# Maxima of the attention scores from 64-row products in pairs, with the decay taken off by VectorE, in the second half of a forgetting attention

## The chip, the cores and the metric

The kernel runs on one core of a Trainium2 chip. A core has five engines with a queue of instructions each: TensorE (matrix products, from SBUF into PSUM), VectorE, ScalarE and GpSimd (elementwise work and reductions), and SyncE, here called SP, which only issues DMA transfers. In the profile they are PE (and PEld for TensorE's loads of the stationary operand), DVE, ACT, POOL and SP. An engine works through its queue in order; a semaphore makes an instruction wait for one of another engine or for a DMA. The metric is device time in microseconds (us) of one execution, as the median of several runs. Everything is float32 outside; products are made in fp32r, with a number split into a high and a low part where more digits are needed.

## The reference

One layer of a hybrid encoder on 2,048 frames plus 16 learned meta tokens (T = 2,064), width 1,024: a normalisation, one input projection, three groups of heads side by side (a gated linear recurrence, a forgetting attention with 8 heads of 64, an RWKV-7 recurrence), an output projection, and a feed-forward part of width 2,816. The change lies in the forgetting attention:

```python
log_f = jax.nn.log_sigmoid(f_logit + f_bias)
c = jnp.cumsum(log_f, axis=1).transpose(0, 2, 1)          # decay, one row a head
s = jnp.einsum('bhqd,bhkd->bhqk', qb, kh) + (cb[..., :, None] - c[..., None, :])
s = jnp.where(kpos[None, :] <= qpos[:, None], s, -jnp.inf)
p = jax.nn.softmax(s, axis=-1)
return jnp.einsum('bhqk,bhkd->bhqd', p, vh)
```

A softmax needs the maximum of each query's row of scores, or a number near it, before the exponentials. The term of the query, cb, is the same for a whole row, so that maximum is the one of (q k - c of the key) over the keys up to the query.

## The kernel before

The stages follow one another: the input projection with the two recurrences beside it, then attention, then the rest of the output projection, then the feed-forward part. The program is traced in Python and a planner (`schedule_with_timeline_sim=True`) then sets the order of each engine's queue by a simulated timeline, the order of the program's text and the buffers that come free; `issue_after` and `add_manual_dep` give it further edges. So instructions of the output projection (tiles `pswo`, lines 172 to 174, three products for each split product) stand between those of attention wherever the planner saw room, as soon as their blocks of 128 frames are ready.

`Attn` (from line 439) works in two halves: blocks 0 and 1 of 512 queries for all 8 heads, then blocks 2 and 3 for all 8 heads. A unit is one head and one block. `run` (line 802) makes a head's keys, then for each block the maxima, and at the same time the weights of the unit two before (AHEAD = 2).

`keys` (line 500) loads for a head: `k1`, 128 rows, the high part of the keys above their low part, and `k2`, the high part in rows 0 to 63, a row of ones (64), and the negative decay as two rows, `ch` and `cl` (65 and 66). In the first half keys number at most `KHALF` = 1,040 and a buffer holds two heads; in the second half a head has 2,064 and fills one of two buffers.

`maxima` (line 530) loads three forms of the block's queries: `q3` (queries in rows 0 to 63, constants 0, 1, 1 in rows 64 to 66, zero below), `q1` (queries twice) and `q2` (their low part, a row for the shift below). For each 128 queries it goes over pieces of keys cut at 0, 400, 912, 1424, 1936 and 2064 (`MAX_CUTS`), up to the last key that these queries may see: one product of `q3` and `k2` over all 128 rows (line 554), which holds the decay by its extra rows; for the last piece a bf16 product that adds the causal mask (line 556); and a VectorE reduction to the maximum of each query (line 559). Block 2 has 13 pieces, block 3 has 17. Then the maxima of a query are joined, turned into a row (line 567) and written negated into row 64 of `q2` (line 568), so that the scores come out shifted.

`weights` (line 649) makes for each 128 keys the scores by two products over 128 rows (lines 681 and 682), the exponential on ScalarE (686), a triangular mask on GpSimd (688), the sums of weights on GpSimd and VectorE (725), and the products with the values (704). These are made in groups of up to eight instructions; each uses 64 of the array's columns (`tile_position=(0, at)`), two of them at the same time, with a manual edge so that both can start together. Between two score tiles `fill` lets as many pieces of the maxima run as their share demands.

PSUM: the maxima, the row transposes and the row totals take turns in three banks in most of the kernel (`mx`, line 493). Loads and stores go through SP's queue, in order.

## Time and profile before

| | |
|---|---|
| median of 3 runs | 3062.89 us (3059.62 to 3063.98) |
| the profiled execution | 3063.42 us, its span 3061.7 us |
| busy, whole span | TensorE 95%, VectorE 67%, ScalarE 48%, GpSimd 45% |
| mean granted TensorE clock | 0.971 |
| reductions to maxima (line 559) | 352, 190.2 us in all |
| products for maxima (line 554) | 352 over both halves |
| value products (line 704) | 704, from 934.6 to 1569.0 us |

The span is from the first to the last instruction. A busy TensorE is not one at its peak: the records of matrix products overlap, so starts are compared where a product's cost matters. A waiting row (A <- B) names the instruction that waited and what ended its wait. "issue" means that the profile shows no engine or transfer that ended it.

### The profile page before, as it was taken

To read this page: it belongs to the slowest core of one execution; us is meant where nothing else is said; L and a number is where in the kernel's file an instruction comes from. 1 tells how busy PE (TensorE), PEld (TensorE's weight loads), DVE (VectorE), ACT (ScalarE), POOL (GpSimd) and SP (SyncE) were. 2 spreads that over 40 slices of the span, in tenths; PEclk is the share of its full clock that TensorE was granted. 3 is DMA by queue.
4 is the path that set the end of the run, shared out by engine and by line. 5 is a ranking of instruction groups with operands and counts; after the bars stand their busy time and mean duration, and the time that the engine had idled before them with its cause. 6 is when DMAs were issued, how large, how long until landed. Compare 5 with 4: busy or idle time off the path is not lost.

```text
span 3061.7 us, 52809 instructions
## 1 busy us (share of the span) xinstructions
PE 2910.2 (95%) x18694; PEld 2487.6 (81%) x18694; DVE 2057.7 (67%) x3934; ACT 1479.1 (48%) x2853; POOL 1365.7 (45%) x1599
## 2 busy tenths in 40 slices
PE   6998999999989999999999899999999999999998
PEld 6997898888876654566568899999999999787786
DVE  5268645656677785555636888888778777547766
ACT  4245332434346554454534656666566665324333
POOL 1001121122214556566843457445645544556765
PEclk8999999999989898999999999999999999999999
DMA  6776478466654347434336555566677765535454
GB/s 216 244 234 207 163 240 292 154 199 205 211 156 92 88 105 211 109 100 122 75 94 206 171 181 180 172 202 213 209 215 212 220 192 165 171 102 175 148 162 145
DMA packets 467750, 532.58 MB, mean 174 GB/s; under 512 B 85550, under 2 KB 355576, under 8 KB 465932
## 3 DMA queue, kind: packets, MB, share of 16 engines
q1 hardware_dynamic: 466716, 528.27, 56.5%
q8 instruction: 147, 2.41, 0.3%
q14 instruction: 119, 0.97, 0.1%
q0 software_dynamic: 768, 0.93, 0.1%
HBM read 369.11 MB, written 159.95 MB: 173 GB/s over the span
## 4 chain that ended last, share of the span: by engine, by line
PE 34%; DVE 5%; DMA 5%; POOL 3%; issue 3%; ACT 1%; SPq 0%; POOLq 0%; DVEq 0%; ACTq 0%
PE psu L172 8%; PE psu L173 8%; PE psu L174 8%; PE psd L172 2%; PE psd L173 2%; PE psd L174 2%; DMA u<-scr_ff 2%; DMA xt<-scr_h 1%; DVE uw L1603 1%; PE pswo L172 1%; PE pswo L174 1%; PE pswo L173 1%; DVE fo L1603 1%; DVE uy L1738 1%; POOL u L1858 1%
## 5 line engine op out<-in xcount | busy, mean ns | idle before, releaser
L172 PE MATMUL psu<-xo,uw 128*128 128x344 f32 x1848 | 590.8, 323 | 14.7 <-DVE vb L1787 6.9
L173 PE MATMUL psu<-xo,uw 128*128 128x344 f32 x1848 | 593.1, 321 | 0.0
L174 PE MATMUL psu<-xo,uw 128*128 128x344 f32 x1848 | 584.3, 320 | 1.5 <-DVE uw L1603 1.5
L172 PE MATMUL psp<-xh,wh 128*128 128x384 f32 (+2 forms) x1152 | 383.5, 333 | 4.5 <-ACT wh L166 3.0
L174 PE MATMUL psp<-xh,wl 128*128 128x384 f32 (+2 forms) x1152 | 379.5, 330 | 2.6 <-DMA wl<-scr_wk 2.5
L173 PE MATMUL psp<-xl,wh 128*128 128x384 f32 (+2 forms) x1152 | 379.3, 329 | 0.0
L1603 DVE TENSOR_TENSOR uw<-uq,uw 128x512 fp32r<-128x512 f32 x341 | 321.0, 947 | 65.1 <-ACT uw L1602 62.8
L172 PEld LDWEIGHTS psu<-xo,uw 128*128 128x128 f32 x1848 | 347.4, 189 | 19.2 <-DVE vb L1787 9.4
L174 PEld LDWEIGHTS psu<-xo,uw 128*128 128x128 f32 x1848 | 347.2, 189 | 2.4 <-DVE uw L1603 2.3
L173 PEld LDWEIGHTS psu<-xo,uw 128*128 128x128 f32 x1848 | 348.5, 189 | 0.1
L1602 ACT ACTIVATE uw<-uq 128x512 fp32r<-128x512 f32 x462 | 287.5, 627 | 107.5 <-PE psu L174 46.6
L686 ACT ACTIVATE p<-sc,bias 128x512 f32<-128x512 f32 (+4 forms) x352 | 197.0, 589 | 194.9 <-PE sc L682 162.1
L559 DVE TENSOR_REDUCE mc<-mx 128x1 f32<-128x512 f32 (+6 forms) x352 | 190.2, 564 | 114.1 <-PE mx L554 87.2
L1738 DVE SCALAR_TENSOR_TENSOR uy<-psu,ffn_cols,uy 128x342 f32<-128x342 f32 (+1 forms) x396 | 223.7, 567 | 62.3 <-ACT uy L1736 60.9
L1744 POOL TENSOR_TENSOR uy<-uy,uy 128x342 f32<-128x342 f32 (+1 forms) x132 | 140.0, 1061 | 252.7 <-DVE uy L1738 70.1
L725 POOL TENSOR_TENSOR acc<-acc,p 128x512 f32<-128x512 f32 (+3 forms) x208 | 221.7, 1068 | 53.1 <-DVE acc L725 23.9
L1603 POOL TENSOR_TENSOR uw<-uq,uw 128x512 fp32r<-128x512 f32 x121 | 177.6, 1468 | 148.0 <-ACT uw L1602 129.5
L172 PEld LDWEIGHTS psp<-xh,wh 128*128 128x128 f32 x1152 | 221.7, 192 | 11.6 <-issue 4.2
L174 PEld LDWEIGHTS psp<-xh,wl 128*128 128x128 f32 x1152 | 220.8, 192 | 12.0 <-issue 5.7
L173 PEld LDWEIGHTS psp<-xl,wh 128*128 128x128 f32 x1152 | 221.3, 192 | 7.5 <-issue 5.4
L1603 DVE TENSOR_TENSOR fo<-u,fo 128x896 fp32r<-128x896 f32 x88 | 109.0, 1240 | 118.8 <-ACT fo L1602 118.8
L1602 ACT ACTIVATE fo<-u 128x896 fp32r<-128x896 f32 x88 | 81.1, 922 | 200.9 <-POOL u L1859 103.8
(470 smaller groups left out, 6470.3 us busy)
## 6 DMA issues: line engine op xcount, KB each, us to landing
uq<-scr_us SPq DMA_DIRECT2D x220, 256.0 KB
uq<-in_ffn_up_dram SPq DMA_DIRECT2D x209, 256.0 KB
wl<-scr_wk SPq DMA_DIRECT2D x48, 512.0 KB
wh<-scr_wk SPq DMA_DIRECT2D x48, 512.0 KB
u<-scr_ff SPq DMA_DIRECT2D x88, 256.0 KB
scr_ff<-uy SPq DMA_DIRECT2D x110, 171.0 KB
raw<-in_w_in_dram SPq DMA_DIRECT2D x24, 512.0 KB
scr_wk<-wh SPq DMA_DIRECT2D x24, 512.0 KB
```

Source lines behind the costliest of these rows:

```text
L172: nc.tensor.matmul(out, ah, bh, start=first, stop=False, skip_group_check=more)
L173: nc.tensor.matmul(out, ah, bl, start=False, stop=False, skip_group_check=more)
L174: nc.tensor.matmul(out, al, bh, start=False, stop=last, skip_group_check=more)
L559: self.reduced = nc.vector.tensor_reduce(mc[:rows, i, ci : ci + 1], ps[:rows, : e - a], axis=AX.X, op=ALU.max)
L686: last = nc.scalar.activation(p[:rows, :w], ps[:rows, :w], AF.Exp, bias=bias[:rows, j : j + 1])
L725: eng.tensor_tensor(a, ps_[0][0][:rows, c0:n] if start and i == 1 else a, p[:rows, : n - c0], op=ALU.add)
L1602: core.nc.scalar.activation(hi, src, AF.Copy)
L1603: (eng or core.nc.vector).tensor_tensor(lo, src, hi, op=ALU.subtract)
L1738: stt(y[:, :n], src[:, i : n + i], cw[:, 44 * i + cc : 44 * i + cc + 1], y[:, :n], op0=ALU.mult, op1=ALU.add)
L1744: core.pooled = nc.gpsimd.tensor_tensor(v[:, :n], g[:, :n], v[:, :n], op=ALU.mult)
L1858: tt(s3, a0, b0, op=ALU.subtract)
```

## The change

In the second half of attention only (keys that number more than 1,040):

- The product for a piece of maxima uses 64 rows: `q1` and `k1` in rows 0 to 63, or `q1` and `k2` in rows 64 to 127, where `k2` now holds the high part of the keys. Two pieces that follow one another form a pair, one on each half of the rows (`tile_position=(lo, 0)`), in two PSUM banks. A manual edge makes the first product of a pair wait also for the reader of the second one's bank. An odd last piece of a block is alone. The mask's product is made behind the pair.
- The decay is no longer part of the product. It is loaded from a new scratch row `c`, the same for all 128 partitions, in three stretches a head (keys 0 to 911, 912 to 1423, 1424 to 2063), and VectorE's reduction becomes `tensor_tensor_reduce`: it subtracts the decay from the PSUM piece, writes it back, and gives the maximum. The first stretch has two places that heads use in turn; the two others have one place each. One of the two places is the room of the three `q3` tiles, which the second half needs no more; the other is a new tile of 1,552 columns.
- `q3` isn't loaded in the second half, and `ch` and `cl` only for the first 1,040 keys. The two later stretches of decay are issued on SP behind the query loads of the head's first block.

In both halves `q2`, `q3` and `k2` have their rows exchanged: the constant rows are 0 to 63, queries and keys 64 to 127. In the first half the pieces are made as before. The output tile of the meta tokens shares a tag with another tile.

```diff
@@ gate_block
+    nc.sync.dma_start(scr["c"][:, t0 : t0 + n], c)
     ch, cl = new("k", F32R), new("r", F32R)
...
+    if t0 < KHALF:
+        w = min(n, KHALF - t0)
+        nc.sync.dma_start(scr["ch"][:, t0 : t0 + w], ch[:, :w].bitcast(F32))
+        nc.sync.dma_start(scr["cl"][:, t0 : t0 + w], cl[:, :w].bitcast(F32))
@@ Attn.mx
         self.bank = (self.bank + 1) % 3 if self.wide else 0
+        self.taken += self.bank != 2
+        self.at = 2 if self.bank == 2 else self.taken % 2
@@ Attn.keys
-        nc.sync.dma_start(k2f[0:64, :n], scr["kh"][r, :n])
-        g = 64 + self.ONES
-        nc.sync.dma_start(k2f[g : g + 1, :n], scr["ch"][h : h + 1, :n])
-        nc.sync.dma_start(k2f[g + 1 : g + 2, :n], scr["cl"][h : h + 1, :n])
+        spans = []
+        if n <= KHALF:
+            nc.sync.dma_start(k2f[1:2, :n], scr["ch"][h : h + 1, :n])
+            nc.sync.dma_start(k2f[2:3, :n], scr["cl"][h : h + 1, :n])
+        else:
+            spans = self.spans(n)
+
+            def span(i):
+                t, a, e = spans[i]
+                nc.sync.dma_start(t, scr["c"][h : h + 1, a:e].broadcast_to([P, e - a]))
+
+            span(0)
+            self.rest.extend(lambda i=i: span(i) for i in range(1, len(spans)))
         nc.sync.dma_start(k1f[0:64, :n], scr["kh"][r, :n])
+        nc.sync.dma_start(k2f[64:128, :n], scr["kh"][r, :n])
         nc.sync.dma_start(k1f[64:128, :n], scr["kl"][r, :n])
...
+    def spans(self, n):
+
+        self.parity ^= 1
+        if not self.decay:
+            own = self.own.tile([P, 1552], F32, tag="decay", name=self.core.n("decay"), bufs=1)
+            self.decay = [self.q3[:].rearrange("p i t -> p (i t)").bitcast(F32), own]
+        homes = (self.parity, 0, 0, 912), (0, 912, 912, 1424), (1, 912, 1424, n)
+        return [(self.decay[i][:, o : o + e - a], a, e) for i, o, a, e in homes]
@@ Attn.maxima
-        nc.sync.dma_start(q3[0:64, :n].bitcast(F32), scr["qh"][r, ts])
+        q3 = None if spans else self.next("q3")
+        if not spans:
+            nc.sync.dma_start(q3[64:128, :n].bitcast(F32), scr["qh"][r, ts])
         nc.sync.dma_start(q1[0:64, :n].bitcast(F32), scr["qh"][r, ts])
         nc.sync.dma_start(q1[64:128, :n].bitcast(F32), scr["qh"][r, ts])
-        nc.sync.dma_start(q2[0:64, :n].bitcast(F32), scr["ql"][r, ts])
+        nc.sync.dma_start(q2[64:128, :n].bitcast(F32), scr["ql"][r, ts])
+        while self.rest:
+            self.rest.pop(0)()
...
+        for g in range(0, len(pieces) if spans else 0, 2):
+            pair, banks, first = [], [], None
+            for piece in pieces[g : g + 2]:
+                pair.append((self.mx(), *piece))
+                banks.append(self.at)
+            for k, lo, (ps, i, ci, a, e, qo, rows, prior) in zip((k1, k2), (0, 64), pair):
+                mm = nc.tensor.matmul(
+                    ps[:rows, : e - a], q1[lo : lo + 64, qo : qo + rows], k[lo : lo + 64, a:e],
+                    start=True, stop=e < prior + rows, tile_position=(lo, 0),
+                )
+                if first is None and len(pair) > 1 and self.readers.get(banks[1]):
+                    core.tc.add_manual_dep(
+                        mm.ins, self.readers[banks[1]],
+                        mybir.DependencyInfo(mybir.DependencyClass.Sync, mybir.DependencyReason.DATA),
+                        reason="both of a pair at the same time",
+                    )
+                first = mm
+            for ps, i, ci, a, e, qo, rows, prior in pair:
+                if e == prior + rows:
+                    nc.tensor.matmul(
+                        ps[:rows, prior - a : e - a], core.identb[:], core.futureb[:], start=False, stop=True
+                    )
+            for at, (ps, i, ci, a, e, qo, rows, prior) in zip(banks, pair):
+                c = next(t[:rows, a - x : e - x] for t, x, y in spans if x <= a < y)
+                self.reduced = nc.vector.tensor_tensor_reduce(
+                    ps[:rows, : e - a], ps[:rows, : e - a], c, 1.0, NEG, ALU.subtract, ALU.max,
+                    mc[:rows, i, ci : ci + 1],
+                )
+                self.readers[at] = self.reduced.ins.name
+            for _ in pair:
+                yield None
...
-        nc.scalar.activation(q2[64:65], ps[0:1], AF.Identity, scale=-1.0, bias=core.ncref[:, ref, h : h + 1])
+        nc.scalar.activation(q2[0:1], ps[0:1], AF.Identity, scale=-1.0, bias=core.ncref[:, ref, h : h + 1])
```

More of the change, by code (lines that the diff above doesn't have):

```diff
@@ L547, in maxima @@
         nc.vector.memset(mc[:], NEG)
-        for i, (qo, rows, prior) in enumerate(qt):
-            for ci in range(len(MAX_CUTS) - 1):
-                a, e = MAX_CUTS[ci], min(MAX_CUTS[ci + 1], prior + rows)
-                if a >= e:
-                    break
-                ps, last = self.mx(), e == prior + rows
-                nc.tensor.matmul(ps[:rows, : e - a], q3[:, qo : qo + rows], k2[:, a:e], start=True, stop=not last)
-                if last:
+        pieces = [
+            (i, ci, x, min(y, prior + rows), qo, rows, prior)
+            for i, (qo, rows, prior) in enumerate(qt)
+            for ci, (x, y) in enumerate(zip(MAX_CUTS, MAX_CUTS[1:])) if x < prior + rows
+        ]
@@ L656, in weights @@
         nc, core, scr = self.nc, self.core, self.scr
-        k1, k2, v1 = keys
+        k1, k2, v1, _ = keys
         q1, q2, bias = queries
@@ L800, with run @@
     AHEAD = 2
-    def run(self, pool):
-        self.queue = self.nc.sync
+    def run(self, pool, own):
+        self.queue, self.own = self.nc.sync, own
         ready = []
@@ L2085, in hybrid_block_kernel @@
             pool(p1b, "pad", 1, **right).tile([P, 24832], F32, name="pad")
-            at.run(pool(p1b, "mt", 1, **right, **early))
+            at.run(*(pool(p1b, s, 1, **right, **early) for s in ("mt", "decay")))
     qp = pool(ctx, "qp", 1, **early)
```

48 lines of the change are left out of this document (27 added, 21 removed).

## The prediction

> **What bounds the kernel now.** I read the page's head first, then the instructions of the value products' line for where attention ends, then the table of windows for its second half (1140 to 1570 us), then the waits of that stretch, then TensorE's instructions in order of time.
>
> ```profile
> span 3061.7 us, 52809 instructions
> ```
>
> ```profile
> L704 PE MATMUL po<-p,v x704: 203/592/1117, 934.6 to 1569.0; 128*64 128x512 f32 x112, 128*64 128x144 f32 x17, 16*64 16x16 f32 x16, 128*64 128x400 f32 x16
> ```
>
> ```profile
> core 0: us, PE busy (x) PEld busy (x) DVE busy (x) ACT busy (x) POOL busy (x), PEclk, DMA share, GB/s
> 1140.00:1215.00 75.00, 66.21 (x306) 34.40 (x305) 45.36 (x100) 33.75 (x62) 39.54 (x47) 0.89 0.74 207
> 1215.00:1300.00 85.00, 81.53 (x362) 48.48 (x361) 45.35 (x92) 38.75 (x71) 52.51 (x74) 1.00 0.48 115
> 1300.00:1450.00 150.00, 143.10 (x648) 90.85 (x647) 85.22 (x181) 74.58 (x137) 100.30 (x141) 0.98 0.44 110
> 1450.00:1570.00 120.00, 112.76 (x504) 62.42 (x502) 62.79 (x113) 64.70 (x117) 94.11 (x111) 0.98 0.25 62
> ```
>
> The windows' rows give a stretch, its length, busy us and instructions of each engine, the granted TensorE clock, and the DMA share and GB/s. The last value product starts at 1569.0 us. In the 430 us TensorE is busy for 66.21 + 81.53 + 143.10 + 112.76 = 403.6 us and shows 26.4 us of idle time. VectorE has 238.7 us of work (56%), GpSimd 286.5 us (67%). TensorE bounds the stage, most tightly from 1215 to 1450, where products of the output projection fill its gaps (224.6 of 235 us).
>
> ```profile
> PEld po L704 <- issue: 44.3, 140, 0.7
> PEld sc L681 <- ACT p L686: 16.4, 39, 1.6
> PEld mx L554 <- DVE mc L559: 16.1, 31, 1.2
> PE mx L554 <- DMA k<-scr_cl: 4.7, 2, 3.0
> PE mx L554 <- DMA k<-scr_kh: 1.8, 1, 1.8
> PE mx L554 <- DVE mc L559: 2.5, 7, 0.8
> ```
>
> Each row: who waited for whom, us in all, times, longest. The engine's own waits for the maxima (16.1 + 2.5 us, for a PSUM bank that VectorE has not yet read) are what the change could shorten. The largest wait, 44.3 us of weight loads before the value products, is put down to "issue", to no other engine. What it is shows in order of time; the columns are start, duration, instruction:
>
> ```profile
> 1400.94 0.40 PE L554 MATMUL mx<-k,q 128*128 128x512 f32 x1
> 1401.18 0.39 PE L172 MATMUL pswo<-woh,mh 128*128 128x512 f32 x1
> ...
> 1402.56 0.35 PE L681 MATMUL sc<-q,k 128*128 128x400 f32 x1
> 1402.74 0.35 PE L682 MATMUL sc<-q,k 128*128 128x400 f32 x1
> ...
> 1417.13 0.39 PE L682 MATMUL sc<-q,k 128*128 128x512 f32 x1
> 1417.45 1.94 PE L704 MATMUL po<-p,v 128*64 128x512 f32 x8
> 1419.32 0.45 PE L554 MATMUL mx<-k,q 128*128 128x400 f32 x1
> 1419.60 0.40 PE L681 MATMUL sc<-q,k 128*128 128x512 f32 x1
> 1419.84 0.40 PE L682 MATMUL sc<-q,k 128*128 128x512 f32 x1
> ```
>
> A maxima product of 512 columns lasts 0.40 us but the next product starts 0.23 to 0.24 us behind it, and 0.18 us behind one of 400. So 0.23 us, not 0.40, is what taking one away saves. Around the value products, which use the array as two column halves, the steps are longer: 0.32 us into them (+0.09), and 0.28 us from the first full product behind them to the next instead of 0.18 (+0.10, its weights were not loaded beforehand).
>
> **The change, part by part.** (1) *Products.* The program has 30 pieces of keys a head in this half (13 for block 2, 17 for block 3), 240 in all. In order they make 14 pairs and 2 singles a head, 112 pairs and 16 singles. If the two of a pair run at once, the shorter one costs nothing: those have 400+256+384+400+400+512 = 2,352 columns in block 2 and 400+256+400+384+400+512+400+512 = 3,264 in block 3, so 8 x 5,616 = 44,928 in all. At 0.23 us for 512: 20.2 us less.
>
> Do they run at once? The recurrent part already has products on 64 rows, both as pairs (line 1112) and alone (line 1037):
>
> ```profile
> 207.22 1.16 PE L1112 MATMUL rps<-rwrav,rwbk 64*128 64x128 f32 x16
> 208.31 0.62 PE L1415 MATMUL eps<-rwlu,lru_ga_w 128*128 128x208 f32 x2
> ...
> 172.98 0.34 PE L172 MATMUL psp<-xh,wh 128*128 128x384 f32 x1
> 173.16 0.34 PE L173 MATMUL psp<-xl,wh 128*128 128x384 f32 x1
> 173.43 1.13 PE L1037 MATMUL eps<-rwwa,wa_up 64*128 64x256 f32 x4
> 174.49 0.44 PE L174 MATMUL psp<-xh,wl 128*128 128x384 f32 x1
> 174.76 0.33 PE L172 MATMUL psp<-xh,wh 128*128 128x384 f32 x1
> ...
> 173.43 0.91 PE L1037 MATMUL eps<-rwwa,wa_up 64*128 64x256 f32 x3
> ```
>
> The first row holds 16 products, 8 pairs, in 1.09 us up to the next product: 0.14 us a pair, way in and out included. One after another, at half of line 1037's 0.22 us for twice the columns (below), they would take 1.76. So pairs do run together, and I take the 20.2 us.
>
> (2) *Going into row halves and out again.* The same rows give its price. In the second group four products take 1.13 us and three 0.91 us, so a further one costs 0.22 us and four 0.88 us. From the last full product before (173.16) to the second one behind (174.76) are 1.60 us. Two full steps (0.18 each, as 172.98 to 173.16) and 0.88 us explain 1.24. The rest, 0.36 us, is the visit: 0.09 us on the way in (0.27 for 0.18), 0.18 us of the group's own first weight load and of the way out (1.06 for 0.88), 0.09 us for the next full product's weight load (0.27 for 0.18). At 0.10 us for each of these two weight loads, as behind the value products, it is 0.39 us, and I take that.
>
> The change makes a visit of every pair and every single, since full products stand around them: 30 pieces a head over 30 score tiles make one pair for each two score tiles, with four full score products between, and the two-bank rule keeps a second pair from following at once. 128 visits x 0.39 = 49.9 us. Those next to the value products, which are a visit already, save one way in or out with its load (half of it, 0.2 us): as at 1419.32, where a maxima product follows directly. I assume 30 of 128, 6.0 us; no view counts this, and bounds are none (49.9 us stays) and all (24.3 us). Sum of (1) and (2): -20.2 + 49.9 - 6.0 = +23.7 us of TensorE time. One pair alone: two products at 0.23 were 0.46 us, now 0.23 + 0.39 = 0.62.
>
> (3) *What of that reaches the end.* TensorE's 26.4 us of idle time can take some: a visit that begins after a wait for a bank or for ScalarE has its way in for nothing. Bounds: nothing, and all 23.7. I take a third, 7.9 us, because in the filled stretch only 10.4 of 235 us are idle. That leaves +15.8 us.
>
> (4) *VectorE.* 240 reductions become subtract-and-reduce with a second operand from SBUF and a write into PSUM.
>
> ```profile
> L559 DVE TENSOR_REDUCE mc<-mx 128x1 f32<-128x512 f32 x125 | 82.6, 680 | 38.0 <-PE mx L554 34.5 <-PE mx L556 2.6
> L1525 DVE SCALAR_TENSOR_TENSOR pswo<-pswo,rs,g_post 128x512 f32<-128x512 f32 x12 | 8.4, 746 | 1.2 <-POOL rs L91 1.2
> L1516 ACT ACTIVATION_READ_ACCUMULATOR jk<-pswo 128x1 f32 x22 | 4.3, 197 | 0.0
> ```
>
> The nearest is line 1525, in place in PSUM with an SBUF operand: 0.746 us against 0.680. 240 x 0.066 = 15.8 us more VectorE work at most, 254.5 of 430 us (59%), hidden behind TensorE; without that cover it would cost 15.8. The lower bound is no change. If the result of the reduction is read out by a separate instruction, as on ScalarE (0.197 us), it is 47 us more, 70% busy with both, still not the bound; only the time a bank stays taken grows.
>
> (5) *Loads.* A head's two 8 KB rows of decay and two 128 KB loads for q3 give way to a decay spread over 128 rows, 128 x 2,064 x 4 = 1,057 KB in three loads, some 6 MB more in all.
>
> ```profile
> q1 hardware_dynamic: 44438, 48.58, 44.0%
> SPq L542 <- PE sc L682: 12.8, 4, 5.7
> ```
>
> The engines' 44% become some 50%, so throughput is no matter. Arrival is: the first pair of a head now needs two copies of the keys and the first stretch of decay, where one copy and the two rows did; the two later stretches wait, on SP's queue, for the previous head's last reduction, with value loads, denominators and the output projection's loads behind them; and each unit's pair reads q1, whose load waits for scores (12.8 us in 4 waits above), instead of q3. Today's waits of maxima for loads are 4.7 + 1.8 us. Bounds: nothing, and three times those, 20 us; I take 5, since the planner sets other work ahead. SP itself issues one load less a head (12 for 13).
>
> (6) *At nothing:* the first half's layout (rows exchanged, same operations), the decay stored once more in each gate block (one small store on SP), the meta tokens' output tile. The cover is TensorE's own work there; without it they are a store and a few fills.
>
> Sum: +15.8 + 5 = +20.8 us on the profiled execution's 3063.4 us (span 3061.7), which is 0.5 us above the runs' median of 3062.9: 3084 us.
>
> **Rivals.** *A: the visits cost nothing, faster.* If the way in and out falls into waits that are there anyway, the gain of (1) alone is left: 3063.4 - 20.2 = 3043 us. For it: 18.6 us of bank waits and 16.4 us for ScalarE stand ready to cover them, 128 visits with at most two hidden loads of 0.10 and two ways of 0.09. Against: the longer steps at 173.16 and 1417.13 follow on steady products, with no wait. It decides if a visit costs under 0.16 us net (20.2 / 128). The Trainium skill's "TensorE: Matmul & The Clock Gate", Measured speedup vs the span model, states that packed products take one product's time and about 4 ns for each further tile; by that model the sum would be this rival's, and it has no term for a lone pair between full products, where the rows show 0.36 us. "TensorEngine Tiling (Array Packing)", Key Properties, states that changing the mode drains the array, which is what the rows look like.
>
> *B: banks.* A pair waits until both its banks of three are read, and one reduction of the pair before is always in between. If each of 112 pairs waits half a reduction more (0.34 us) and today's 18.6 us go, it adds 19.5 us to the forecast: 3104 us. For it: 31 + 7 such waits today with one bank a product. Against: a pair comes every 430/120 = 3.6 us and two reductions take 1.36. The skill's "VectorE: DVE Perf Modes", Two Vector instructions with no wait between them, counts an operation that writes its accumulator out as two instructions, which would lengthen this occupation; no row here shows it on VectorE.
>
> *C: the two halves do not run at once* (other bank or port limits at 512 columns): without the 20.2 us, 3084 + 20 = 3104 us. Against: line 1112.
>
> *D: swallowed:* the idle 26.4 us take the 23.7, and the loads are hidden: 3063 us. Against: only 10.4 us of it lies in the filled stretch.
>
> **How the numbers follow.** Forecast 0.55, A 0.20, B 0.10, C 0.05, D 0.10. What a measurement of this kernel can tell is about 0.2%, 6 us: faster 0.20 (A), same 0.10 (D), slower 0.70. The forecast's own range: low, all visits shared and a third absorbed, with no load cost, (-20.2 + 24.3) x 2/3 = +2.7, 3066; high, nothing shared or absorbed and 20 us of loads, +49.7, 3113. The range takes in B, C and D and the larger part of A: 3046 to 3114.
>
> **What would show it.** Right: maxima products as 64*128 with starts of a pair together, the step out of a pair and the next full product's step each about 0.1 us long, weight loads of full products "issue"-waiting behind pairs, TensorE's time from the first to the last value product up by 15 to 30 us, VectorE's operation 0.68 to 0.75 us. Wrong: attention's second half ends earlier than 1569 us while the tail behind it is unchanged (A), or bank waits of more than 40 us (B), or pairs with starts 0.2 us apart (C). The prediction falls if the planner puts several pairs behind one another or mostly beside value products.

## The result, and the profile after

The changed kernel takes 3107.5 us (median of 4 runs, 3099.8 to 3111.8), the kernel before on the same chip 3061.3 us: a ratio of 1.0151, with a 95% interval of 1.0137 to 1.0165. It is slower by 46 us, where 21 were forecast (3084 us); the range to 3114 holds it. The profiled execution took 3108.2 us. Its page begins:

```profile
span 3106.5 us, 53171 instructions
```

Then the instructions of the value products' line (767 now), with first and last start; before, the last was at 1569.0 us:

```profile
L767 PE MATMUL po<-p,v x704: 204/592/1116, 936.1 to 1608.8; 128*64 128x512 f32 x112, 128*64 128x144 f32 x18, 16*64 16x16 f32 x16, 128*64 128x400 f32 x16
```

So 40 of the 45 us of span were lost before the end of attention. I cut attention at starts of score products, which come in the same number in both kernels (704): the first one; the 225th, the first of the second half; the 245th; and the last value product. In us of the two profiled executions, with TensorE's granted clock (its mean over the stretch, as a share of full speed):

| | before | after | difference | clock before | clock after |
|---|---|---|---|---|---|
| up to the first score product | 903.8 | 905.5 | +1.7 | 0.965 | 0.971 |
| to the 225th | 239.8 | 253.1 | +13.3 | 0.896 | 0.846 |
| 225th to 245th (change of halves) | 29.3 | 25.5 | -3.8 | 0.825 | 0.733 |
| 245th to the last value product | 396.1 | 424.6 | +28.5 | 0.978 | 0.956 |
| behind it | 1492.7 | 1497.7 | +5.0 | 0.987 | 0.986 |

So the clock is lower in all three stretches of attention, and about the same outside it.

The windows of after (columns as in the prediction) show how the long stage goes:

```profile
1215.00:1300.00 85.00, 77.63 (x324) 39.44 (x323) 45.37 (x119) 36.14 (x68) 50.28 (x68) 0.92 0.44 108
1300.00:1450.00 150.00, 147.87 (x647) 86.31 (x645) 80.65 (x241) 70.56 (x131) 91.44 (x140) 1.00 0.49 128
1450.00:1610.00 160.00, 145.75 (x612) 69.85 (x611) 85.93 (x233) 78.47 (x140) 109.99 (x132) 0.96 0.30 71
```

From 1300 to 1450 TensorE is busy for 147.87 of 150 us at a granted clock of 1.00 and holds 647 instructions; in before this stretch held 648 in 143.10 busy us. The gaps are filled, yet no more is done. In TensorE's order of time a pair looks like this:

```profile
1428.81 0.39 PE L745 MATMUL sc<-q,k 128*128 128x512 f32 x1
1429.04 0.40 PE L174 MATMUL pswo<-woh,ml 128*128 128x512 f32 x1
1429.36 0.50 PE L601 MATMUL mx<-k,q 64*128 64x512 f32 x2
1429.79 0.50 PE L744 MATMUL sc<-q,k 128*128 128x512 f32 x1
1430.13 0.40 PE L745 MATMUL sc<-q,k 128*128 128x512 f32 x1
```

The row with x2 is a pair: two products of 512 columns lie within 0.50 us. But the step into it is 0.32 us, the step out 0.43 and the next full product's 0.34, where each is 0.23 among full products. The pair saves one step of 0.23 and adds 0.09 + 0.20 + 0.11 = 0.40 us. Its waits, and VectorE's new operations (a group's busy us, mean ns of one, idle time before it). A wait can stand both in the product's row (PE) and in that of its weight load (PEld), as here the 6.5 us for `q`, so the two rows are not added:

```profile
PE mx L601 <- DVE mc L619: 13.6, 19, 2.0
PE mx L601 <- DMA q<-scr_qh: 6.9, 2, 6.5
PEld mx L601 <- DVE mc L619: 26.3, 41, 2.2
PEld mx L601 <- issue: 24.8, 57, 1.6
PEld sc L744 <- issue: 18.7, 49, 1.6
PEld mx L601 <- DMA q<-scr_qh: 7.4, 2, 6.5
```
```profile
L619 DVE CUSTOM_DVE_ANT_0 mx<-mx,q 128x512 f32<-128x512 f32 x79 | 55.6, 708 | 34.9 <-PE mx L601 34.7
L619 DVE DVE_READ_ACCUMULATOR2_ANT mc<- 128x1 f32 x230 | 32.0, 139 | 0.0
```

The second operation is 0.708 us long where the reduction was 0.680, and a read of the accumulator of 0.139 us stands behind each one. PEld's waits for "issue" before score products and before the maxima's own products were these before the change:

```profile
PEld sc L681 <- issue: 11.7, 18, 1.1
PEld mx L554 <- issue: 10.0, 13, 3.4
```

I read the 31 more of the first kind and the 44 more of the second as weight loads that were not made beforehand, behind pairs and on the way into them.

### The profile page after: what moved, and what is told of

The parts are those of the page before. It is cut to its first block, busy times and chain, and to the rows that moved or that the text cites. A ratio compares the mean times of both kernels' runs of the same rounds, so it can differ in the third digit from the quotient of the medians.

```text
span 3106.5 us, 53171 instructions
## 1 busy us (share of the span) xinstructions
PE 2945.0 (95%) x18694; PEld 2481.0 (80%) x18694; DVE 2059.7 (66%) x4168; ACT 1477.8 (48%) x2853; POOL 1349.0 (43%) x1599
## 5 line engine op out<-in xcount | busy, mean ns | idle before, releaser
L1665 ACT ACTIVATE uw<-uq 128x512 fp32r<-128x512 f32 x462 | 287.4, 627 | 103.5 <-PE psu L174 51.0
L767 PE MATMUL po<-p,v 128*64 128x512 f32 (+4 forms) x704 | 170.4, 563 | 0.0
```

The source lines that it names most:

```text
L767: mm = nc.tensor.matmul(po[at : at + 64, c0:n], v1[:rows, j], p[:rows, : n - c0], start=start and i < 2, stop=end and i + 2 >= len(group), ...
L1665: core.nc.scalar.activation(hi, src, AF.Copy)
```

## The experiments

"To the 245th" runs from the first score product, "rest" from the 245th to the last value product, and "clock" is the mean granted clock in the rest, all from the profiled execution; ratios are to the kernel before on the same chip. Medians of different rows come from different chips, on which the kernel before took 3061 to 3072 us.

| kernel | median | ratio (95%) | to 225th | to 245th | rest | clock |
|---|---|---|---|---|---|---|
| before | 3061.3 | 1 | 239.8 | 269.1 | 396.1 | 0.978 |
| after | 3107.5 | 1.0151 (1.0137-1.0165) | 253.1 | 278.7 | 424.6 | 0.956 |
| zero_decay | 3067.1 | 0.9991 (0.9973-1.0009) | 241.9 | 274.8 | 387.7 | 0.991 |
| zero_loads | 3161.0 | 1.0301 (1.0284-1.0318) | 240.3 | 275.0 | 322.5 | 0.968 |
| zero_spread | 3069.1 | 0.9996 (0.9978-1.0015) | 241.0 | 274.4 | 386.7 | 0.991 |
| full_rows | 3088.4 | 1.0046 (1.0020-1.0071) | 249.1 | 275.2 | 412.0 | 0.959 |
| full_alone | 3090.0 | 1.0071 (1.0036-1.0106) | 247.8 | 280.5 | 406.0 | 0.975 |
| full_alone_q1 | 3077.3 | 1.0049 (1.0031-1.0068) | 248.6 | 282.9 | 398.2 | 0.979 |
| halves_alone | 3141.6 | 1.0250 (1.0213-1.0287) | 245.7 | 270.7 | 459.0 | 0.937 |
| no_edge | 3124.4 | 1.0175 (1.0150-1.0200) | 255.4 | 283.4 | 439.6 | 0.957 |
| q1_four | 3100.0 | 1.0111 (1.0082-1.0140) | 247.9 | 277.2 | 423.7 | 0.956 |
| layout_only | 3076.2 | 1.0029 (1.0011-1.0046) | 243.3 | 272.8 | 395.3 | 0.987 |
| load_order | 3106.7 | 1.0119 (1.0082-1.0156) | 256.4 | 284.0 | 426.2 | 0.952 |
| store_all | 3107.7 | 1.0132 (1.0102-1.0162) | 246.0 | 276.6 | 428.2 | 0.952 |
| first_half | 3106.6 | 1.0137 (1.0111-1.0163) | 238.3 | 278.8 | 423.4 | 0.960 |
| both | 3097.9 | 1.0108 (1.0080-1.0136) | 237.1 | 278.1 | 427.2 | 0.948 |
| full_first | 3088.9 | 1.0062 (1.0047-1.0077) | 239.8 | 275.5 | 413.4 | 0.967 |
| q3_first | 3112.6 | 1.0145 (1.0117-1.0173) | 235.5 | 279.6 | 425.5 | 0.960 |
| q3_both | 3116.8 | 1.0154 (1.0119-1.0189) | 243.7 | 287.4 | 427.8 | 0.952 |
| q3_after | 3104.9 | 1.0122 (1.0093-1.0150) | 247.9 | 277.9 | 426.0 | 0.952 |

**Row halves against full rows.** full_rows takes the halves away and keeps all else; its maxima then also hold the product with the keys' low part, which `k1` carries in rows 64 to 127. full_alone takes away the pairs too, and halves_alone the pairs alone.

```diff
 # full_rows
-  ps[:rows, : e - a], q1[lo : lo + 64, qo : qo + rows], k[lo : lo + 64, a:e],
-  start=True, stop=e < prior + rows, tile_position=(lo, 0),
+  ps[:rows, : e - a], q1[:, qo : qo + rows], k1[:, a:e], start=True, stop=e < prior + rows,
 # full_alone: full_rows and this; halves_alone: the changed kernel and this
-  for g in range(0, len(pieces) if spans else 0, 2):
-      for piece in pieces[g : g + 2]:
+  for g in range(len(pieces) if spans else 0):
+      for piece in pieces[g : g + 1]:
```

> The changed kernel with each product of the second half made over all 128 rows of q1 and k1 (which adds the keys' low part to the maxima), so without row halves; pairs of banks, the edge between them, the loads and VectorE's subtract-and-reduce stay. Theory visits (TensorE pays for going into row halves and out): the changed kernel has 137 visits, 31 of them beside value products, 137 x 0.39 - 31 x 0.2 = 47 us, and gains 20 by pairing; so 27 us come back, about 3080 us. Rival banks and VectorE (two banks a pair, a longer reduction): nothing comes back, and the products at full price add up to 20 us: 3107 to 3127 us.

> As full_rows (all 128 rows of q1 and k1, no row halves), and each product by itself: no pairs and no edge between their banks. full_rows lies 13 us above the unchanged second half. Theory pairs of banks: most of it comes back, 3066 + 10 = 3078 us (the first half's order keeps its 10). Rival: VectorE's longer operation or the loads of decay and q1 cost it: 3088 us as full_rows.

> The changed kernel with every product of the second half alone on one row half, none in pairs, so no edge either. Theory visits: 200 to 240 visits instead of 137 and the pairing's 20 us given up; at 0.39 us, with those beside value products at 0.2, some 25 to 40 us for the visits: 3150 to 3165 us if it all reaches the end, 3135 if two thirds do. Rival banks: what costs is the wait for two banks, which is gone: 3107 us or less.

With full rows the rest of attention is 412.0 and 406.0 us, with pairs 424.6, with lone halves 459.0. So row halves cost 13 to 19 us with pairs and 47 to 53 without. Whole executions say the same, or a little more: q1_four and full_alone_q1 (below), which differ by row halves and pairs alone and ran on one chip, have medians 22.7 us apart, and the ratios of after and the two full kernels differ by 0.80 and 1.05%, some 25 and 32 us, each uncertain by some 10 us. full_rows waits for VectorE's banks as after does, without row halves:

```profile
PE mx L601 <- DVE mc L618: 13.6, 20, 2.0
PEld mx L601 <- DVE mc L618: 23.5, 34, 2.2
PE mx L601 <- DMA q<-scr_qh: 3.3, 2, 2.4
```

full_alone's two bank rows are 1.0 and 12.3 us, yet its ratio is no lower than full_rows'. In halves_alone the way in and out looks as it does around a pair; here a lone product of 400 columns:

```profile
1405.68 0.40 PE L744 MATMUL sc<-q,k 128*128 128x512 f32 x1
1405.91 0.40 PE L745 MATMUL sc<-q,k 128*128 128x512 f32 x1
1406.24 0.45 PE L601 MATMUL mx<-k,q 64*128 64x400 f32 x1
1406.62 0.50 PE L744 MATMUL sc<-q,k 128*128 128x512 f32 x1
1406.96 0.39 PE L745 MATMUL sc<-q,k 128*128 128x512 f32 x1
```

From 1405.91 to 1406.96 are 1.05 us; two full steps of 0.23 and the product's 0.18 make 0.64, and the visit 0.41 us. In TensorE's order of time halves_alone has 170 visits, 33 of them next to value products, and the changed kernel 137 (82 of one pair, 46 of a single product, 9 longer), 31 next to value products. By the prediction's prices, halves_alone should lose 170 x 0.39 - 33 x 0.2 = 60 us and shows 47 to 53; the changed kernel 137 x 0.39 - 31 x 0.2 - 20.2 = 27 and shows 13 to 19.

**The edge of a pair.** no_edge leaves out the manual dependency.

```diff
-                if first is None and len(pair) > 1 and self.readers.get(banks[1]):
-                    core.tc.add_manual_dep(...)
```

> The changed kernel without the manual edge that makes a pair's first product wait for the second one's bank. Theory visits: no gain; pairs come apart a little more often, each 0.2 to 0.6 us: 3105 to 3125 us. Rival banks: the waits for VectorE that the edge makes (27 us of weight loads wait for reductions in the changed kernel, 16 before) shrink, 3090 to 3100 us.

The products' waits for VectorE all but go (0.9 us for after's 13.6), and the weight loads' fall (15.3 for 26.3):

```profile
PE mx L601 <- DVE mc L613: 0.9, 3, 0.3
PEld mx L601 <- issue: 44.8, 83, 5.5
PEld mx L601 <- DVE mc L613: 15.3, 37, 0.8
```

But now 127 visits are of single products and 32 of two, 175 in all, and the rest is 439.6 us, 15 us longer (the medians differ by 17 us; the ratios by 0.24%, with intervals that overlap). In this kernel waiting for both banks cost less than taking pairs apart.

**VectorE's operation and the spread loads.** zero_decay computes as before (decay in the product) with the changed layout, and lets VectorE subtract a tile of zeros. zero_spread loads these zeros as the changed kernel loads the decay. Nothing is left out in either.

```diff
 # zero_decay, second half
-  nc.vector.tensor_reduce(mc[:rows, i, ci : ci + 1], ps[:rows, : e - a], axis=AX.X, op=ALU.max)
+  nc.vector.tensor_tensor_reduce(ps[:rows, : e - a], ps[:rows, : e - a], zeros[:rows, : e - a],
+      1.0, NEG, ALU.subtract, ALU.max, mc[:rows, i, ci : ci + 1])
 # zero_spread: zeros loaded in stretches of 400 (two places in turn), 512, 512 and 640 keys
+  nc.sync.dma_start(t, scr["z"][h : h + 1, a:e].broadcast_to([P, e - a]))
```

> As layout_only, with VectorE's subtract-and-reduce in the second half instead of the plain reduction, subtracting a tile of zeros that is never loaded (the decay stays in the product). Theory VectorE: the operation and the read of its accumulator (0.71 + 0.14 us for 0.68 in the changed kernel's profile) hold the banks longer: 240 times 0.17 is 41 us of VectorE, and 5 to 13 us reach the end: 3081 to 3089 us against layout_only's 3076. Rival loads: VectorE has room, nothing reaches the end: 3076 us within 5.

> The zero_decay kernel, in which VectorE subtracts one zero tile of 512 columns that is never loaded; here the zeros come from a scratch row, spread over 128 rows in three loads a head, with the places, the order on SP and the turns of the changed kernel. Nothing of the computation is left out. Theory L (the spread loads themselves, and the waits at their places, are the 18 us between zero_decay's second half, 420.6 us, and full_alone's, 438.7): second half 433 to 442 us, about 3083 us. Theory Q (it is q1's late load and the missing q3, the spread loads lie beside other work): second half 418 to 426 us, about 3067 us.

> zero_loads again with less room: in it the larger tiles made the planner put the output projection's products behind attention (second half 357 us, behind it 259 instead of 113), so it told nothing of the loads. Here the first place holds 400 keys, two in turn, and there are four loads a head (400, 512, 512 and 640 keys, the same bytes as in the changed kernel), and the output projection's products stand in attention as in before. Beside zero_decay this adds the spread loads alone; nothing is left out. Theory L (the spread loads and the waits at their places are the 18 us): second half 433 to 442 us, total about 3083 us. Theory Q (q1's late load is): second half 418 to 426 us, total about 3067 us.

The operation costs nothing at the end (ratio 0.9991, rest 387.7 against 396.1). zero_loads gave no answer: with its larger tiles the planner put the output projection's products behind attention, 48 instead of 384 of them before the last value product, and the median is 94 us above zero_decay's, most likely what filling attention's gaps is worth here. With them in place (zero_spread) the loads cost nothing either: ratio 0.9996, rest 386.7 us, though VectorE does wait for them:

```profile
L603 DVE CUSTOM_DVE_ANT_0 mx<-mx,decay 128x512 f32<-128x512 f32 x128 | 88.3, 707 | 60.8 <-PE mx L596 40.3 <-DMA decay<-scr_z 13.5 <-PE mx L598 6.8
```

So the 19 us between zero_spread's rest (386.7) and full_alone's (406.0) are neither VectorE's work nor the decay's bytes.

**The queries' load.** What differs between those two in the product is its operands, `q1` and `k1` in place of `q3` and `k2`; besides that, the stretches and their places, the decay rows' stores and loads, and the order that the planner made of it all. `q1` belongs also to the scores, so its load waits until the scores of three units before are done. full_alone_q1 and q1_four give every fourth unit of the second half a buffer of its own; both is q1_four on top of first_half (below).

```diff
-        q1 = self.t([P, 512], "q1", F32R, self.AHEAD + 1)
+        self.units = getattr(self, "units", 0) + bool(spans)
+        if self.units and self.units % 4 == 0:
+            q1 = self.own.tile([P, 512], F32R, tag="q1x", name=core.n("q1"), bufs=1)
+        else:
+            q1 = self.t([P, 512], "q1", F32R, self.AHEAD + 1)
```

> As full_alone (128 rows of q1 and k1, each product by itself), with the fourth buffer of q1. Theory q1: 10 to 15 of the 18 us that its second half takes longer than zero_decay's come back: 3075 to 3080 us against full_alone's 3090. Rival: decay loads and the third key load: 3090 us.

> The changed kernel with a fourth buffer of q1 in the second half (2 KB, taken from the filler tile beside it); the first half's order is the same. Theory q1: the pairs read q1, whose load waits for the scores of three units before, and pairs wait for it (7 us of waits in the changed kernel's second half, 18 in full_alone); with a fourth buffer the load goes out a unit earlier: 5 to 10 us back, 3097 to 3102 us. Rival: the decay's loads on SP's queue, not q1: 3107 us.

> first_half and q1_four together: the row halves, pairs and VectorE's operation stay, the first half's order and the early q1 are mended. If the theories hold, the two add up: 3107 - 13 - 8 = 3086 us, which leaves the visits and the decay's loads, 15 to 25 us above the kernel before. Rival: only one of the two comes back, 3095 to 3100 us.

TensorE's waits of maxima for loads, in full_alone and then in full_alone_q1:

```profile
PE mx L601 <- DMA q<-scr_qh: 18.4, 5, 4.5
PEld mx L601 <- DMA q<-scr_qh: 9.4, 3, 4.9
```
```profile
PE mx L605 <- DMA k<-scr_kl: 9.4, 3, 3.4
PEld mx L605 <- DMA k<-scr_kl: 3.9, 1, 3.9
```

The wait for the queries goes and the rest falls from 406.0 to 398.2. The medians differ by 13 us, but they come from two chips: the ratio falls from 1.0071 to 1.0049, within the intervals. What is late next is the keys' low part, which only the full products of these kernels read. With pairs it is the second copy of the keys; q1_four shows:

```profile
PE mx L605 <- DMA k<-scr_kh: 4.3, 2, 3.7
PEld mx L605 <- DMA k<-scr_kh: 5.5, 2, 4.2
```

It takes the place of after's rows for the queries, and the rest is 423.7 us for 424.6. q1_four's ratio is lower by 0.4%, about 12 us, and of that only 2.4 us lie in the profiled attention.

The theory of `q1` is not borne out in full. In the four kernels with the fourth buffer, attention from its first score product to its last value product changes by -2.4 us (q1_four), -5.5 (full_alone_q1), +3.1 (both, against first_half) and +10.1 (q3_both, against q3_first). both takes 3097.9 us where 3086 were expected if the two cures added up.

**The first half.** Its operations are as before, yet it took 13 us longer. layout_only keeps the new layout, the store of `c` and the order of loads, and computes the second half as before. load_order restores the order of the key loads in the first half, store_all the full store of `ch` and `cl`, first_half both.

```diff
 # layout_only: the first branch for every n; store_all and first_half: ch, cl stored for all T
-        if n <= KHALF:
+        if True:
-    if t0 < KHALF:
+    if True:
 # load_order and first_half, keys of the first half
+            nc.sync.dma_start(k2f[64:128, :n], scr["kh"][r, :n])   # ahead of ch and cl
```

> The changed kernel with the second half made as the first: products over all 128 rows of q3 and k2 with the decay in them, plain reductions, decay rows for all keys; what stays of the change is the exchange of rows, q3 as one tile, the order of the key loads and the extra store of c. Theory first half: the 13 us that attention's first half lost in the changed kernel come from these, and the second half is as before: 3061 + 13 = 3074 us, more if the second half suffers from the order of loads too. Rival: they come from the second half's code, by the plan that it makes or its early loads: 3061 us, within 6.

> The changed kernel with the high part of the keys for k2 loaded first in the first half, as before the change, where the change put it behind the two decay rows and the first copy for k1. Theory: the first half's 13 us are its products waiting for this load; they come back: 3095 us. Rival: they are the planner's other order or the fills of q3: 3107 us.

> The changed kernel with the decay rows ch and cl stored for all keys again, as before the change (the second half does not read them). With that the planner sets TensorE's queue through attention's first half as in the kernel that kept only the layout, which lost 3.5 us there and not 13. Theory order: the first half's loss is the planner's other order, set off by the gate blocks' stores; about 10 us come back: 3097 us. Rival: it comes from the second half's loads or buffers that are asked for early: 3107 us.

> The changed kernel with two things of the first half as before the change: ch and cl stored for all keys, and the keys' high part for k2 loaded first. With both, the planner sets TensorE's queue in attention's first half as in the kernel before (with the first alone it did not). Theory order: the first half takes 240 us again instead of 253, and all in all some 13 us come back: 3094 us, with a few us of doubt for the second half's order, which changes too. Rival: the first half's loss comes from what the second half loads early, or from a clock state: 3107 us.

Alone, load_order and store_all leave the total where it was, within the noise. Both together put TensorE's planned order in the first half back to that of before (all but a few instructions), and it takes 238.3 us again. So what was lost there comes with another order of the queues, set off by small edits to loads and stores, and from no operation. Its size is known less well than a single pair of profiles suggests: the nine kernels with nearly the changed kernel's order there (after, the three full ones with it, halves_alone, no_edge, q1_four, load_order, q3_after) take 245.7 to 256.4 us, the six with the order of before 235.5 to 243.7, so some 11 us between the means. And it shows as granted clock: 0.846 in after, 0.896 in before, 0.910 in first_half; the time multiplied by the clock is 214, 215 and 217 us. But the total does not fall: the next 20 score products take 40.5 us in place of 25.5, and the 245th stands at 278.8 us, after's place (278.7). There the trace of first_half shows, on TensorE and VectorE (the brackets give idle time and what ended it):

```profile
1147.06 0.77 PE L748 MATMUL sc<-q,k 128*128 128x512 f32 x2
1153.80 0.70 PE L605 MATMUL mx<-k,q 64*128 64x256 f32 x2 [5.97 <-DVE mc L623]
```
```profile
1153.06 0.58 DVE L623 CUSTOM_DVE_ANT_0 mx<-mx,decay 128x400 f32<-128x400 f32 x1 [6.93 <-DMA decay<-scr_c]
```
```profile
1145.27 0.39 SPq L1401 DMA_DIRECT2D scr_mix<-rwxu  x1
1146.45 0.45 SPq L538 DMA_DIRECT2D k<-scr_kh  x1
1146.95 0.58 SPq L533 DMA_DIRECT2D decay<-scr_c  x1
```

The second half's first stretch of decay is issued on SP behind the last store of the recurrent part (`rwxu`), and TensorE waits 6 us for the bank that VectorE cannot read without it. full_first asks whether this debt needs pairs (it is full_alone with first_half's edits). q3_first begins the two places of the first stretch the other way round, so that the load need not wait for room that the recurrent part holds; q3_both has the fourth q1 buffer besides, and q3_after is that edit on the changed kernel.

```diff
-        self.rest, self.parity, self.decay = [], 0, []
+        self.rest, self.parity, self.decay = [], 1, []
```

> The full_alone kernel (products of 128 rows one at a time, decay by VectorE) with the gate block's stores and the first half's key loads as in the kernel before, so with the first half's queues in the order of before, as in first_half. full_alone took 247.8 us in the first half, 438.7 in the second, 3090.0 us in all. Theory S (what the first half regains is a debt that the second half pays whatever its products are, for example loads or output projection work that has to be done there instead): first half about 238, second half about 449, total 3087 to 3093. Theory P (in first_half it was the pairs' bank waits under another plan that took it away): first half about 238, second half 436 to 441, total about 3080.

> first_half with the turn of the first stretch's two places begun the other way: the second half's first head takes the room of the three q3 tiles, which is free after the first half's last maxima product, where it took the new tile, whose room the recurrent part beside attention holds to its end. Theory R (the transition between the halves: the first stretch of decay stands on SP behind the recurrent part's last store, and the second half's first pieces wait for it, which eats what the first half regained): VectorE's wait of 6.9 us for the decay goes, first half about 238 us, second half 450 to 457 instead of 463.9, total 3093 to 3100 us. Theory O (the debt is elsewhere, in the output projection's order or the scores'): first half about 238, second half 462 to 466, total 3104 to 3109 us.

> q3_first with a fourth q1 buffer for every fourth unit, as in both (468.2 us in the second half, 3097.9 us in all). Theory R: the second half at 450 to 460, total 3083 to 3092 us. Theory O: 466 to 470, total 3096 to 3100 us.

> The changed kernel with the turn of the two places begun the other way, as in q3_first, and nothing else. In the changed kernel the decay is in time (its transition shows no wait for it), since the first half is late. Both theories: first half 250 to 256, second half 447 to 452, total 3102 to 3110 us; if it gains as much as q3_first does, theory R is not what makes the difference.

full_first regains 8 us to the 225th, still has 5 of them at the 245th, loses 7.4 in the rest and ends where full_alone did (3088.9 us for 3090.0): pairs are not needed for the debt, and it is not always paid at the same place. The theory of the late decay fell. In q3_first the stretch was issued at 1131 us, 15 us earlier, and the 245th score product stands at 279.6 us all the same; other loads of the same queue were late in its place:

```profile
DVE mx L623 <- DMA decay<-scr_c: 14.8, 1, 14.8
PE mx L671 <- DMA mt<-scr_cl: 13.4, 1, 13.4
```

The first is now a later stretch of decay, the second the meta tokens' loads. q3_both gained nothing (ratio 1.0154), and q3_after lies where both theories had it. What sets the place of the 245th stays open. In the nine kernels with row halves in pairs kept by the edge, it comes 42 to 45 us after SP issues the recurrent part's last store, early or late (233.9 and 278.7 us from the first score product in after, 236.5 and 278.8 in first_half, 239.5 and 284.0 in load_order, 244.1 and 287.4 in q3_both). That would point to the end of the recurrent part, which shortening attention's first half does not bring nearer. But in the other kernels the distance is 28 us (before) to 50 us (zero_loads), so it is no fixed one, and it was not tried apart.

## Why the prediction was right in sign and too small

The steps on the row halves held. What failed is (5) and (6), which put the rest of the loss at 5 us and at nothing, and the sum's silence on the granted clock. From the first to the last value product TensorE takes 38 us more, where 15 to 30 were to show that the forecast was right. That the range held the result is no merit of its reasons: its upper end is the case of nothing absorbed and 20 us of loads.

*(1) The pairs run together:* right; x2 rows of 0.50 us, where a lone product of 512 columns takes 0.48 in halves_alone. Taking pairing away (halves_alone) costs 34.4 us of rest, where 20.2 and 33 more visits at 0.39 make 33.1; that leaves nothing for the third that (3) lets idle time take.

*(2) The price of a visit:* right, 0.40 us around the pair shown and 0.41 around the lone product, for 0.39. There were 137 visits and not 128, 31 beside value products for 30.

*(3) Two thirds reach the end, +15.8:* right in size; 13 to 19 us between pairs and full rows in the profiles, 23 between the medians on one chip. Rival A falls: among steady full products nothing hid the visits. The Trainium skill's "TensorE: Matmul & The Clock Gate", Measured speedup vs the span model, has the pair itself right (two products in about one's time, here 0.50 us), but no term for the way in and out, which the rows have at 0.40. C falls by the x2 rows, D by the result. B's sign seems to appear, 13.6 and 26.3 us of bank waits, just under its bound of 40, but the two rows are for the most part the same waits. Counted once they are 27 us, for 16 before, so the prediction's 18.6 counts some twice as well. full_rows has 25 us of them and in all is no slower than full_alone with 12, so B falls too; and without the edge that makes them the rest is 15 us longer (no_edge).

*(4) VectorE hidden:* right; the price lies within the bounds named, 0.03 us more an operation and a read of 0.139 us behind it, and zero_decay shows that it costs nothing at the end. The Trainium skill's "VectorE: DVE Perf Modes", Two Vector instructions with no wait between them, which counts such an operation as two, holds on VectorE in this trace: 230 reads in the window shown.

*(5) Loads, +5:* this step failed, in its size and in its mechanism. What is left when the row halves are taken away is 21 us and not 5, a little over the upper bound of 20: attention from its first score product to its last value product takes 665.3 us before, 686.5 in full_alone and 687.1 in full_rows (by the ratios the two are some 22 and 14 us slower than before, with the whole program counted). The 6 MB more of decay and its later stretches are not the cause: with the spread loads alone it takes 661.1 us (zero_spread). Nor does late arrival explain it. In the second half the changed kernel's products for maxima wait 6.9 us for loads, where before's waited 4.7 + 1.8, and full_rows' 3.3. Kernels whose products are made alone wait longer, full_alone 18.4 us for `q1`, whose load waits behind the scores as the prediction's row of 12.8 us said; but the fourth buffer that takes this wait away returns 5.5 us there and 2.4 in the changed kernel. That the planner would set other work ahead may have been the wrong guess; no run shows it. So the 21 us are shown, and their cause stays open in the main.

*(6) At nothing:* this step failed as well. The first half lost 13 us in the profiled execution, not by its operations but with the planner's other order, which I had taken for fixed. It was not the place where the total was set either, since returning it changed nothing. Up to the 245th score product the change costs 9.6 us; layout_only has 3.7 of these, and its median is 0.29% above before (0.11 to 0.46%), which zero_decay and zero_spread, with the same layout, do not repeat.

*A term that the sum lacks: the granted clock.* The prediction read it in the windows' rows and then priced every step as if it stayed. The times of attention's three stretches, each multiplied by its clock, add up to 626.4 us before and 638.7 after, so as an estimate from these traces at most some 26 of its 38 us go with the lower clock. It is the most, since waits for loads or other engines need not get longer with a slower TensorE. By this estimate all of the first half's loss is of this kind (215 us before, 214 after), and some 10 of the 28.5 us of the rest; of the rest's other 18, 10 to 11 lie between after and the full kernels, and 7 to 8 between these and before. It is no accident of the profiled execution: the clock of the whole span is 0.964 to 0.966 in the changed kernel's four runs and 0.970 to 0.979 in all runs of the kernel before. How much of it the waits cause, and how much the order, no run separates.

The changed kernel's 38 us of attention are 16.8 between after and full_alone and 21.2 between full_alone and before, against 15.8 and 5. Of the other 6.7 us outside attention no run gives a cause: the time behind the last value product is 1492.6 to 1499.7 us over all kernels but zero_loads, without an order that follows the edits.

No version beat the kernel before; the nearest, zero_decay and zero_spread, are the new layout without the row halves, and are level with it.

## What to carry to other kernels

A lone pair of row halves between full products saved one product's step (0.23 us) and paid 0.40 us for the steps into it, out of it and behind it: price such a change by the number of visits, not of products. To put several pairs behind one another, where banks allow it, would follow from that, but no run here tried it. When an operand is replaced by one that serves another stage as well, look up which work its buffer waits for, since that wait moves to the new reader; and test whether removing the wait returns its time, which here it mostly did not. Where a planner sets the order, a small edit to loads or stores can move a stage by some 10 us, and larger tiles moved the end by 94: compare the kernels at a point behind which both are in the same state, and see whether what one stage regains is still there at that point. And read the granted clock stage by stage beside the times, before a difference is put down to waits or work.

## What the runs showed of the hardware that was not expected

A pair of 512 columns and a lone 64-row product of 400 both take a step of some 0.4 us out (0.43 and 0.38), for 0.23 and 0.18 among full products: 0.20 us more in both cases, whether one product is inside or two.

And where TensorE idles, the granted clock is lower behind it. In the changed kernel a product for maxima waits 6.45 us for its queries, to 1245.98 us; from within this wait to 7 us behind it the clock is half, and in the 228 us that follow, in which TensorE is 98% busy, it is full. First the row of TensorE's timeline, then the two windows:

```profile
1245.98 0.70 PE L601 MATMUL mx<-k,q 64*128 64x400 f32 x1 [6.45 <-DMA q<-scr_qh]
1243.10:1253.10 10.00, 6.71 (x15) 3.50 (x17) 3.56 (x12) 2.58 (x4) 4.26 (x6) 0.50 0.76 150
1253.30:1481.80 228.50, 222.94 (x971) 125.21 (x967) 127.66 (x367) 112.10 (x206) 144.76 (x213) 1.00 0.45 115
```

In first_half, at the change of halves, it is busy for 4.97 of 13 us, and the granted clock (the third number from the end) is 0.60 there and 0.50 in the 15 us that follow:

```profile
1147.00:1160.00 13.00, 4.97 (x13) 2.12 (x13) 5.05 (x17) 0.59 (x3) 0.89 (x5) 0.60 0.70 142
1160.00:1175.00 15.00, 11.96 (x40) 4.87 (x41) 11.15 (x40) 2.43 (x5) 1.71 (x2) 0.50 0.56 133
```

In the kernel before the same place has 9.24 of 14 us and 0.77, then 0.88:

```profile
1144.00:1158.00 14.00, 9.24 (x36) 3.44 (x34) 6.33 (x20) 2.49 (x6) 2.45 (x5) 0.77 0.73 136
1158.00:1173.00 15.00, 13.95 (x70) 7.69 (x71) 9.15 (x20) 8.45 (x14) 8.55 (x10) 0.88 0.64 153
```

That is likely one reason why the same 20 score products take 40.5 us there and 29.3 before; how much of it the clock makes was not measured apart. These stretches go together with the idle time in them, but no run set the one without the other.
